# A hybrid decoder trunk on one core: input scaled chunk by chunk, time steps from the normalised input, the residual transposed in eight later jobs

## The chip, the cores and the metric

The kernel runs on one core of a Trainium2 chip. TensorE (PE) multiplies and transposes, VectorE (DVE), ScalarE (ACT) and GpSimd (POOL) work elementwise, and SyncE (SP) issues most of the DMA transfers; sixteen DMA engines carry them. The metric is the device time of one execution in microseconds.

## The reference

The trunk has two layers; only the first is touched. It adds 16 learned meta tokens in front of 1024 tokens (together 1040) of width 1024, normalises, and runs a state-space mixer:

```
h = jnp.concatenate([meta_tokens, x], axis=1)
u = h * rsqrt(mean(h * h) + 1e-6) * ssd_norm
z, xbc, dt_raw = jnp.split(u @ w_in, [2048, 2048 + 3072], axis=-1)
xbc = jax.nn.silu(_causal_dwconv(xbc, conv_w, conv_b))
xs, b_in, c_in = jnp.split(xbc, [2048, 2048 + 512], axis=-1)
dt = jax.nn.softplus(dt_raw + dt_bias)
a_cs = cumsum(dt * -exp(a_log))
y = ssd(xs, b_in, c_in, dt, a_cs)        # 32 heads in 4 groups, by chunks
h = h + gated_norm(y + xs * d_skip, z) @ w_out
```

A convolutional feed-forward block, a stick-breaking attention with one shared key and value, and a second feed-forward block follow, then a final normalisation that drops the meta tokens.

## The kernel before

Activations lie transposed: features on the 128 partitions (eight blocks, `KD`), tokens along the free axis. Tokens come in nine chunks `CH` of 116 (the last 112), and three token tiles `TT` of 348, 348 and 344, so one tile is three chunks. A product of fp32 operands is three float32r products of split operands (`mm3`, L193 high by high, L194 high weights by low input, L195 low weights by high input). `load_w` loads a 128x1024 block of weights on SyncE's queue (L174) into a buffer tagged `w32`, ScalarE rounds it to the high part `wh` (L180), GpSimd makes the low part `wl` in pieces (L98). All three tags rotate among three buffers.

`load_x` is the front. It starts the loads of the nine chunks, alternately on ScalarE's and SyncE's queue, and of the time-step weights, which GpSimd multiplies by the gain of the norm (L349). `stream(j)` handles the raw tile j: sums of squares (L364 on VectorE, L366 on ScalarE), raw transposes `xT` (L371) of three chunks for each feature block, copies of them into the residual `h` (L374, L376), a plain fp32 product `dtr` of time-step weights and raw residual (L377), and for the last tile the stores of eight residual blocks to HBM, `h_d` (L379). `token_rstd` makes the tile's factors 1/rms (L244 to L250). `scaled(j)` multiplies the chunks by the factors (L388), transposes them again (`xr`, L393) and splits them into the high and low parts `uh` (L303, ScalarE) and `ul` (L304, VectorE). `ORD` gives the program's order, tile by tile: `stream(j)`, then `scaled(j)`.

`dt_path` then finishes the time steps, multiplying the raw product by the factors at L460, and works out the decays. Its last step writes cumulated decays and their exponentials as rows to HBM, `acs_d` and `ea_d` (L499), from where each chunk of the state-space part loads them spread over partitions: `D` (L637, 116 partitions) and `E` (L643, 128 partitions).

`in_group(0)` projects the first group: six blocks of 128 columns (four of x, one of B, one of C), each for three token tiles, so 18 projections `pj` of 24 products, each followed by a convolution of four taps (L320 ScalarE, L323 VectorE) and a Silu (L512). `self.stream` walks through blocks and tiles and asks for a block's weights one block ahead. Up to here a list scheduler with a simulated timeline sets the order on each engine, from the program's dependences and tile pools; DMA issues stand on SyncE in the order it finds and one behind another, a waiting one in front of all later ones. From the next line on (`manual_schedule` in `mixer`) the order is written by hand. The first instructions of that part on TensorE are the transposes `cb` (L665) of chunk 0; they mark the end of the region that the change touches. The residual stored at the front is read again after the mixer.

Of the kernel before, what the change touches and what calls it, by code (L numbers as in the profile page):

```python
# [13 lines left out]
P = 128  # L14
# [54 lines left out]
LPOOL = ((2, 2), (2, 4), (2, 6), (2, 7))  # L69
ORD = ((0, 0), (1, 0), (0, 1), (1, 1), (0, 2), (1, 2))  # L70
XB, SQD = 9, (1, 4, 7)
# [29 lines left out]
class Trunk:  # L101
    def __init__(self, ctx, tc, a):
        self.tc, self.nc, self.a = tc, tc.nc, a
        nc = self.nc
        self.cp = ctx.enter_context(tc.tile_pool(name="cp", bufs=1))
        self.qp = ctx.enter_context(tc.tile_pool(name="qp", bufs=NQ))
        self.tmps = ctx.enter_context(tc.tile_pool(name="up", bufs=8))
        self.wp = ctx.enter_context(tc.tile_pool(name="wp", bufs=3))
        self.mp = ctx.enter_context(tc.tile_pool(name="mp", bufs=2, space=bass.MemoryType.PSUM))
        self.sp = ctx.enter_context(tc.tile_pool(name="sp", bufs=SMB, space=bass.MemoryType.PSUM))  # L110
        self.dp = ctx.enter_context(tc.tile_pool(name="dp", bufs=1, space=bass.MemoryType.DRAM))
        self.n = 0
        self.open = []
        self.consts()

# [55 lines left out]
    def load_w(self, src, n, gain=None, out=None):  # L171
# [7 lines left out]
        wh, wl = out or [self.wp.tile([P, 1024], F32R, tag=t, name=self.nm(t)) for t in ("wh", "wl")]  # L179
        nc.scalar.activation(wh[:, :n], w32[:, :n], AF.Copy)  # L180
        pieces(nc.gpsimd, wl[:, :n], w32[:, :n], wh[:, :n].bitcast(F32), ALU.subtract)
# [8 lines left out]
    def mm3(self, out, wh, wl, uh, ul, first, last, joins=False, tie=None):  # L190

        mm = self.nc.tensor.matmul
        self.behind(mm(out, wh, uh, start=first, stop=False, skip_group_check=joins), tie, "behind the sums of squares")  # L193
        mm(out, wh, ul, start=False, stop=False, skip_group_check=joins)  # L194
        mm(out, wl, uh, start=False, stop=last, skip_group_check=joins)  # L195

# [40 lines left out]
    def token_rstd(self, ss, m, k, eps=EPS, y=None, src=None):  # L237
# [3 lines left out]
        if y is None:  # L241
            y = self.small("ty")
            self.ln_exp()
        nc.vector.tensor_scalar(ss[:m, :k], (ss if src is None else src)[:m, :k], 1.0 / D, eps, op0=ALU.mult, op1=ALU.add)  # L244
        nc.scalar.activation(y[:m, :k], ss[:m, :k], AF.Ln)
        nc.scalar.activation(y[:m, :k], y[:m, :k], AF.Exp, scale=-0.5)
        nc.vector.tensor_tensor(b[:m, :k], y[:m, :k], y[:m, :k], op=ALU.mult)
# [47 lines left out]
    def parts(self, t, u, s0, n, g, eng=None):  # L295
# [6 lines left out]
        else:  # L302
            nc.scalar.activation(h, t, AF.Copy, scale=g)  # L303
            nc.vector.scalar_tensor_tensor(l, t, g, h.bitcast(F32), op0=ALU.mult, op1=ALU.subtract)  # L304

# [20 lines left out]

    def load_x(self, pool, mx):

# [3 lines left out]
        nc.vector.memset(ss, 1.0)  # L332
        wdt = self.wp.tile([P, 1024], F32, tag="w32", name="wdt")
        self.ln_exp()
        d = self.dp.tile([KD, P, L], F32, tag="h0_d", name="h0_d")
        r9 = mx.tile([P, 3, 3], F32, tag="r9", name="r9")
        dt = self.ex("dtr")
        xs = []
        for c, (t0, n) in enumerate(CH):
            xt = pool.tile([P, D], F32, tag="x", name=self.nm("x"), bufs=XB)  # L340
# [3 lines left out]
            else:  # L344
                self.by_rows(nc.sync if c % 2 else nc.scalar, xt[:n, :], a["x"][t0 - META : t0 - META + n, :], n)
            if c == 0:
                nc.sync.dma_start(wdt[:, : KD * H], a["w_dt"])
                v = wdt[:, : KD * H].rearrange("p (k h) -> p k h", k=KD)
                nc.gpsimd.tensor_tensor(v, v, self.par("ssd_norm", 0, KD).unsqueeze(2).to_broadcast([P, KD, H]), op=ALU.mult)  # L349
# [4 lines left out]
        hs = [self.Q("h") for _ in range(KD)]  # L354

        def stream(j):
            s0, nn = TT[j]
            x3 = xs[3 * j : 3 * j + 3]
            for i in range(3):
                c = 3 * j + i  # L360
                n = CH[c][1]
                t = self.wp.tile([P, D], F32, tag="wl", name=self.nm("junk"))
                if c in SQD:
                    nc.vector.scalar_tensor_tensor(t[:n, :], x3[i][:n, :], 1.0, x3[i][:n, :], op0=ALU.mult, op1=ALU.mult, accum_out=ss[:n, c : c + 1])  # L364
                else:
                    nc.scalar.activation(t[:n, :], x3[i][:n, :], AF.Square, accum_out=ss[:n, c : c + 1])  # L366
            for k in range(KD):
                ps = self.lg("xT")
                for i in range(3):
                    n = CH[3 * j + i][1]  # L370
                    nc.tensor.transpose(ps[:, i * CB : i * CB + n], x3[i][:n, k * P : k * P + P], self.ident[:n, :n])  # L371
                h = hs[k][:, s0 : s0 + nn]
                if k % 2:
                    nc.scalar.activation(h, ps[:, :nn], AF.Copy)  # L374
                else:
                    nc.vector.tensor_copy(h, ps[:, :nn])  # L376
# [3 lines left out]
            self.token_rstd(ss[:, 3 * j : 3 * j + 3], CB, 3, y=r9[:, :, j])  # L380

        def scaled(j):
            s0, nn = TT[j]
            x3 = xs[3 * j : 3 * j + 3]
            for i, t in enumerate(x3):
                n = CH[3 * j + i][1]
                r = r9[:n, i : i + 1, j]
                nc.vector.tensor_scalar(t[:n, :], t[:n, :], r, None, op0=ALU.mult)  # L388
            for k in range(KD):
                ps = self.sm("xr")  # L390
                for i in range(3):
                    n = CH[3 * j + i][1]
                    nc.tensor.transpose(ps[:, i * CB : i * CB + n], x3[i][:n, k * P : k * P + P], self.ident[:n, :n])  # L393
                self.parts(ps[:, :nn], u[k], s0, nn, self.par("ssd_norm", k))

        for step, j in ORD:
            (scaled if step else stream)(j)
        return d, u, dt, r9

# [33 lines left out]

    def dt_path(self, ps, r9, cp):

        nc, a = self.nc, self.a
        H, C = HEADS, 9 * HEADS
        heads = cp.tile([P, 2, H], F32, tag="heads", name="heads")
        nc.gpsimd.dma_start(heads.rearrange("p i h -> p (i h)"), a["heads"].to_broadcast([P, 2 * H]))
        aneg = heads[:, 1]  # L440
        self.tc.keep_in_program_order(nc.scalar.activation(aneg, aneg, AF.Exp))
        nc.vector.tensor_scalar(aneg, aneg, -1.0, None, op0=ALU.mult)

# [59 lines left out]
    def in_block(self, u, col, cv, out):  # L503
# [3 lines left out]
        def tile(w, j):  # L507
# [3 lines left out]
            self.conv(ps, t, n, 4, HALO, lambda i: self.par("ssd_conv_w", cv * 4 + i), self.par("ssd_conv_b", cv), self.settle)  # L511
            self.open.append(lambda: nc.scalar.activation(t, t, AF.Silu))  # L512

# [83 lines left out]
    def settle(self):  # L597

        todo, self.open = self.open, []
        for f in todo:  # L600
            f()

    def stream(self, blocks, w0=None):

# [10 lines left out]
        for n in range(3 * len(todo)):  # L615
            i, j = divmod(n, 3)
            if j == 0:
                if i + 1 < len(todo):
                    w.append(self.load_w(todo[i + 1][0], D))
                cur = w.pop(0)  # L620
            if n in calls:
                calls.pop(n)()
# [96 lines left out]
    def mixer(self, mx):  # L719


        with self.tc.tile_pool(name="start", bufs=3) as pool:
            hd, u, *dt = self.load_x(pool, mx)
            dt = self.dt_path(*dt, mx)
        with self.tc.tile_pool(name="ssd", bufs=3) as pool:
            yd, rows = [None] * 4, [[] for _ in range(4)]
            accs = [{} for _ in range(4)]
# [25 lines left out]
            with self.tc.manual_schedule(engines={E.PE, E.DVE, E.Activation, E.Pool}):  # L753
# [42 lines left out]
                for _ in work:  # L796
                    pass
        return hd, rows[3][:4], yd, list(zip(y0[1], y0[0]))

# [1031 lines left out]
```

## Time and profile before

| | us |
|---|---|
| median of 3 runs | 2890.64 |
| lowest and highest run | 2889.72, 2891.4 |
| the profiled execution | 2892.33 |
| its span | 2890.5 |

| instant in the profiled execution | us |
|---|---|
| first transpose of the input | 5.78 |
| first projection (L193) | 32.78 |
| transposes of the decay rows (L493) | 99.74 |
| first load of `D` issued | 103.59 |
| first transpose of the state-space part (L665) | 131.18 |

The profile is of one execution. A timeline row has the start, the length, the engine, line and operation, output and inputs, shapes and the number of instructions merged in the row, and in brackets the idle time of the engine before it and what ended it. A group row has the busy time and the mean ns of one instruction. SPq and ACTq rows are issues of DMA transfers; a row that merges several lasts from the first to the last.

### The profile page before, as it was taken

How to read it: one execution, taken by the hardware profiler on the slowest of the kernel's cores; microseconds unless marked ns; L12 is line 12 of the kernel's file. 1: busy time of each engine (PE TensorE's matmuls, PEld its weight loads, DVE VectorE, ACT ScalarE, POOL GpSimd, SP SyncE). 2: the span in 40 equal slices, each digit the busy share in tenths (PEclk: the TensorE clock that was granted, in tenths of full speed). 3: DMA queues.
4: the chain of work that ended last, by engine and by line, in shares of the span. 5: the costliest groups of instructions: out<-in, count | busy, mean ns of one | idle time of the engine just before them, and what ended most of it. 6: DMA issues, size and time to landing. Idle time of an engine off the chain costs nothing. (4 is left out here: it accounts for less than half of the span.)

```text
span 2890.5 us, 58592 instructions
## 1 busy us (share of the span) xinstructions
PE 2834.6 (98%) x21835; PEld 2701.9 (93%) x21835; DVE 2096.3 (73%) x4044; ACT 1628.0 (56%) x3392; POOL 1610.4 (56%) x2430
## 2 busy tenths in 40 slices
PE   7999999999999999999999999999999999999998
PEld 4999999999999999999999999999798999999888
DVE  5676666668387667666886888888749776767776
ACT  4455544544265656565335888888736565555433
POOL 2265555552429888858743222222363888885882
PEclk9999999999999999999999999999999999999999
DMA  5233333343213222244132222222332222225331
GB/s 168 75 107 95 117 94 117 114 156 135 81 60 97 81 81 76 81 161 164 52 114 78 57 68 66 62 63 54 134 117 74 81 76 79 81 81 183 110 102 66
DMA packets 128265, 278.70 MB, mean 96 GB/s; under 512 B 14787, under 2 KB 58828, under 8 KB 127980
## 3 DMA queue, kind: packets, MB, share of 16 engines
q1 hardware_dynamic: 122028, 261.70, 28.7%
q10 hardware_dynamic: 4112, 6.56, 0.7%
q0 software_dynamic: 1840, 6.70, 0.6%
q8 instruction: 172, 2.82, 0.4%
q14 instruction: 113, 0.93, 0.1%
HBM read 204.63 MB, written 55.36 MB: 90 GB/s over the span
## 5 line engine op out<-in xcount | busy, mean ns | idle before, releaser
L98 POOL TENSOR_TENSOR wl<-w,wh 128x256 fp32r<-128x256 f32 x768 | 682.0, 918 | 377.3 <-ACT wh L180 299.8
L193 PE MATMUL pj<-uh,wh 128*128 128x348 f32 (+2 forms) x1536 | 500.0, 326 | 2.7 <-DVE qs L1469 1.9
L194 PE MATMUL pj<-ul,wh 128*128 128x348 f32 (+2 forms) x1536 | 494.7, 322 | 0.0
L195 PE MATMUL pj<-uh,wl 128*128 128x348 f32 (+2 forms) x1536 | 491.5, 320 | 0.0
L193 PE MATMUL p<-bh,fh 128*128 128x262 f32 (+1 forms) x1408 | 400.4, 285 | 5.5 <-DVE p L1118 5.5
L195 PE MATMUL p<-bh,fl 128*128 128x262 f32 (+1 forms) x1408 | 400.1, 284 | 1.9 <-POOL fl L98 1.9
L194 PE MATMUL p<-bl,fh 128*128 128x262 f32 (+1 forms) x1408 | 398.7, 283 | 0.0
L98 POOL TENSOR_TENSOR fl<-x,fh 128x256 fp32r<-128x256 f32 x352 | 265.6, 786 | 191.9 <-ACT fh L1055 161.5
L193 PE MATMUL p<-bh,wh 128*128 128x262 f32 (+1 forms) x1040 | 295.7, 284 | 1.5 <-ACT ft L1115 1.5
L194 PE MATMUL p<-bl,wh 128*128 128x262 f32 (+1 forms) x1040 | 295.8, 284 | 1.2 <-DVE bl L979 1.2
L195 PE MATMUL p<-bh,wl 128*128 128x262 f32 (+1 forms) x1040 | 295.0, 284 | 0.0
L193 PEld LDWEIGHTS pj<-uh,wh 128*128 128x128 f32 x1536 | 288.3, 188 | 5.0 <-issue 1.9
L194 PEld LDWEIGHTS pj<-ul,wh 128*128 128x128 f32 x1536 | 288.9, 188 | 1.1
L195 PEld LDWEIGHTS pj<-uh,wl 128*128 128x128 f32 x1536 | 288.6, 188 | 0.6 <-issue 0.6
L323 DVE SCALAR_TENSOR_TENSOR c<-p,params,c 128x260 f32<-128x260 f32 (+1 forms) x528 | 248.5, 480 | 53.3 <-ACT c L320 46.7
L193 PEld LDWEIGHTS p<-bh,fh 128*128 128x128 f32 x1408 | 267.1, 190 | 6.3 <-DVE p L1118 5.9
L195 PEld LDWEIGHTS p<-bh,fl 128*128 128x128 f32 x1408 | 267.0, 190 | 2.8 <-POOL fl L98 2.5
L194 PEld LDWEIGHTS p<-bl,fh 128*128 128x128 f32 x1408 | 267.5, 190 | 0.1
L1115 ACT ACTIVATE ft<-p 128x262 f32<-128x262 f32 (+1 forms) x352 | 132.5, 382 | 175.0 <-DVE p L1118 111.2
L195 PE MATMUL acc<-gh,wl 128*128 128x260 f32 (+1 forms) x672 | 213.5, 320 | 2.8 <-POOL wl L98 2.6
L193 PE MATMUL acc<-gh,wh 128*128 128x260 f32 (+1 forms) x672 | 210.9, 320 | 3.1 <-DVE h L1279 3.1
L194 PE MATMUL acc<-gl,wh 128*128 128x260 f32 (+1 forms) x672 | 213.9, 319 | 0.0
(332 smaller groups left out, 7898.9 us busy)
## 6 DMA issues: line engine op xcount, KB each, us to landing
w<-in_w_up SPq DMA_DIRECT2D x88, 512.0 KB
w<-in_w_down SPq DMA_DIRECT2D x44, 512.0 KB
w<-in_w_in SPq DMA_DIRECT2D x40, 512.0 KB
E<-ea_d SPq DMA_DIRECT2D x32, 464.0 KB
D<-acs_d SPq DMA_DIRECT2D x32, 420.5 KB
g<-c SPq DMA_DIRECT2D x88, 130.0 KB
g<-c SPq DMA_DIRECT2D x88, 128.0 KB
b<-g SPq DMA_DIRECT2D x16, 520.0 KB
```

Of the source, the lines that this page charges most:

```text
L98: eng.tensor_tensor(out[:, c], x[:, c], y[:, c], op=op)
L193: self.behind(mm(out, wh, uh, start=first, stop=False, skip_group_check=joins), tie, "behind the sums of squares")
L194: mm(out, wh, ul, start=False, stop=False, skip_group_check=joins)
L195: mm(out, wl, uh, start=False, stop=last, skip_group_check=joins)
L323: ins = nc.vector.scalar_tensor_tensor(out, ps[:, o + i : o + i + n], wcol(i), out, op0=ALU.mult, op1=ALU.add)
L1115: nc.scalar.activation(s[:, :N], ps[:, :N], AF.Copy)
```

## The change

- The loads of the input stand on SyncE's queue but for chunks 0 and 2, which ScalarE issues. The first weight block is loaded between chunk 1 and the time-step weights.
- `tile(j)` takes the place of `stream` and `scaled`: the sums of squares of a chunk, factors of the first two chunks of a tile and then of the third, scaling chunk by chunk (the last chunk half on VectorE, half on ScalarE), transposes and parts. Squares of the next tile stand between the transposes of this one.
- Raw transposes, their copies into `h`, the plain product `dtr`, the gain on the time-step weights, the eight early stores and the multiplication by factors in `dt_path` go.
- The time steps come from the normalised parts by `mm3`, 24 triples of 96 columns with padded weights `wd`, in one bank.
- The meta tokens' columns of the residual are transposed at the start and stored.
- `residual(f)` makes the other 1024 columns of feature block f: it loads column block f of the input as 128x8x128 into a `w32` buffer, transposes eight times, copies the two banks back into the same buffer on ScalarE, and stores them to HBM. Eight such jobs are called, one after each of the projections 3, 5, ... 17 (counted from zero).
- The first three projections are interleaved with the tiles; some ties (`hold`, `copy_tie`, `silu_tie`, `last_mm`) only order instructions of one engine. The second block's weights are asked for one tile later.

```diff
-        for c, (t0, n) in enumerate(CH):
+        def load(c):
...
-                self.by_rows(nc.sync if c % 2 else nc.scalar, xt[:n, :], a["x"][t0 - META : t0 - META + n, :], n)
+                self.by_rows(nc.scalar if c == 2 else nc.sync, xt[:n, :], a["x"][t0 - META : t0 - META + n, :], n)
...
+        for c in range(3):
+            load(c)
+        w32 = self.wp.tile([P, 1024], F32, tag="w32", name="w32_0")
+        nc.sync.dma_start(w32, first)
...
+        nc.sync.dma_start(wdt, a["w_dt"])
+        for c in range(3, 9):
+            load(c)
...
+        def tile(j):
+            a, b, c = range(3 * j, 3 * j + 3)
+            if j == 0:
+                for x in (a, b, c):
+                    square(x, None)
+            factors(j, 0, 2)
+            scale(a, [(nc.vector, 0, D)])
+            factors(j, 2, 1)
+            scale(b, [(nc.scalar if j else nc.vector, 0, D)], None if j else self.first_factor)
+            if j == 0:
+                self.behind(nc.scalar.activation(w0[0], w32, AF.Copy), self.last_exp, "behind the factors")
+                pieces(nc.gpsimd, w0[1], w32, w0[0].bitcast(F32), ALU.subtract)
+            scale(c, [(nc.vector, 0, D // 2), (nc.scalar, D // 2, D)])
+            transposed(j, range(KD // 2))
...
+            transposed(j, range(KD // 2, KD))
...
-                nc.tensor.matmul(dt[j * H : j * H + H, :nn], wdt[:, k * H : k * H + H], h, start=k == 0, stop=k == KD - 1)
-                if j == 2:
-                    nc.sync.dma_start(d[k], hs[k][:, :L])
...
+                    self.mm3(dt[:G, :n], wd[0][:, w], wd[1][:, w], u[k][0][:, c], u[k][1][:, c], j == k == 0, j == 2 and k == KD - 1, tie=self.last_mm)
...
+    def residual(self, f):
+        nc = self.nc
+        t = self.wp.tile([P, 1024], F32, tag="w32", name=self.nm("xb"))
+        nc.sync.dma_start(t.rearrange("p (c q) -> p c q", q=P), self.a["x"][:, f * P : f * P + P].rearrange("(c p) q -> p c q", p=P))
+        banks = [self.sm("xT") for _ in range(2)]
+        for c in range(SEQ // P):
+            nc.tensor.transpose(banks[c // 4][:, c % 4 * P : c % 4 * P + P], t[:, c * P : c * P + P], self.ident)
+        for i, ps in enumerate(banks):
+            nc.scalar.activation(t[:, 512 * i : 512 * i + 512], ps, AF.Copy)
+        nc.sync.dma_start(self.h0_d[f, :, META:], t)
...
-        tt(v3, pv[R].rearrange("p (c h) -> p c h", h=H), r9[:CB].rearrange("p i j -> p (i j)").unsqueeze(2).to_broadcast([CB, 9, H]), op=ALU.mult)
-        tt(v3, v3, bias, op=ALU.add)
+        tt(v3, pv[R].rearrange("p (c h) -> p c h", h=H), bias, op=ALU.add)
...
-            for n, _ in enumerate(self.stream(into(0))):
+            blocks_left = iter(range(KD))
+            for n, _ in enumerate(group, 3):
+                if n % 2:
+                    for f in islice(blocks_left, 1):
+                        self.residual(f)
```

On SyncE, before, the loads of `D` and `E` and the weights behind the decay rows stand so (`w_176`, `w_196`, `w_223` are weights of later groups):

```order
L499 DMA acs_d<-rows_642 32x3x116 x3
L499 DMA ea_d<-ea_889 32x3x116 x3
L637 DMA D_1201<-acs_d 116x928
L637 DMA D_1299<-acs_d 116x928
L643 DMA E_1301<-ea_d 128x928
L174 DMA w_176_1384<-in_w_in 128x1024
L637 DMA D_1424<-acs_d 116x928
L643 DMA E_1426<-ea_d 128x928
L174 DMA w_196_1550<-in_w_in 128x1024
L174 DMA w_223_1770<-in_w_in 128x1024
```

In the changed kernel the same stretch of SyncE holds three residual loads (`xb_1098` to `xb_1258`, the sixth to the eighth), stores of residual blocks, and weights (`w_125` of the group's last block, `w_135` of the first block of the next group):

```order
L174 DMA w_125_1028<-in_w_in 128x1024
L707 DMA D_1276<-acs_d 116x928
L471 DMA h_d<-xb_938 128x1024
L707 DMA D_1374<-acs_d 116x928
L713 DMA E_1376<-ea_d 128x928
L707 DMA D_1499<-acs_d 116x928
L471 DMA h_d<-xb_1013 128x1024
L713 DMA E_1501<-ea_d 128x928
L465 DMA xb_1098<-in_x 128x8x128
L174 DMA w_135_1143<-in_w_in 128x1024
L465 DMA xb_1183<-in_x 128x8x128
L471 DMA h_d<-xb_1098 128x1024
```

The loads of the decay rows, which stood behind weights fetched earlier, now stand ahead of the sixth residual load and of the weights that the last projection before the state-space part uses.

On TensorE, before, the last projection ends and the state-space part begins:

```order
L193 MATMUL pj_1213<-uh_151,wh_1100 128x352
L194 MATMUL pj_1213<-ul_152,wh_1100 128x352
L195 MATMUL pj_1213<-uh_151,wl_1101 128x352
L665 MATMUL cb_1251<-ident,xbc_1007 116x128
L666 MATMUL cb_1251<-xbc_1107,xbc_1007 116x116
```

In the changed kernel the last projection (`pj_1288`) begins behind the transposes of the sixth residual load and holds those of the seventh:

```order
L195 MATMUL pj_1228<-uh_153,wl_1031 128x348
L468 MATMUL xT_1100<-ident,xb_1098 128x128 x4
L468 MATMUL xT_1101<-ident,xb_1098 128x128 x4
L193 MATMUL pj_1288<-uh_139,wh_1145 128x352
L194 MATMUL pj_1288<-ul_140,wh_1145 128x352
L468 MATMUL xT_1185<-ident,xb_1183 128x128 x4
L195 MATMUL pj_1288<-uh_139,wl_1146 128x352
```

and it ends with those of the eighth, in front of the first transpose of the state-space part:

```order
L194 MATMUL pj_1288<-ul_154,wh_1145 128x352
L195 MATMUL pj_1288<-uh_153,wl_1146 128x352
L468 MATMUL xT_1260<-ident,xb_1258 128x128 x4
L468 MATMUL xT_1261<-ident,xb_1258 128x128 x4
L735 MATMUL cb_1326<-ident,xbc_1037 116x128
```

Three of the eight residual jobs have thus moved in among the last rows ahead of the state-space part.

More of the change, by code (lines that the diff above doesn't have):

```diff
@@ L179, in load_w @@
         wh, wl = out or [self.wp.tile([P, 1024], F32R, tag=t, name=self.nm(t)) for t in ("wh", "wl")]
-        nc.scalar.activation(wh[:, :n], w32[:, :n], AF.Copy)
+        self.behind(nc.scalar.activation(wh[:, :n], w32[:, :n], AF.Copy), self.copy_tie, "behind the tiles in front")
         pieces(nc.gpsimd, wl[:, :n], w32[:, :n], wh[:, :n].bitcast(F32), ALU.subtract)
@@ L194, in mm3 @@
         mm(out, wh, ul, start=False, stop=False, skip_group_check=joins)
-        mm(out, wl, uh, start=False, stop=last, skip_group_check=joins)
+        self.last_mm = mm(out, wl, uh, start=False, stop=last, skip_group_check=joins)
     def split(self, t, s, eng=None, tiles=TT):
@@ L382, in scaled @@
[L382 to L394, printed above, removed]
@@ L396, in load_x, with square @@
-        for step, j in ORD:
-            (scaled if step else stream)(j)
-        return d, u, dt, r9
+        G = 3 * H
+        wd = [self.Q("wd", F32R) for _ in range(2)]
+        for t in wd:
+            nc.gpsimd.memset(t.bitcast(F32), 0.0)
+        taps = [t[:, 2 * H : 2 * H + KD * G].rearrange("p (k h) -> p k h", h=G)[:, :, :H] for t in wd]
+        made = {}
+        def square(c, tie):
+            n = CH[c][1]
+            t = self.wp.tile([P, D], F32, tag="wl", name=self.nm("junk"))
+            x, acc = xs[c][:n, :], ss[:n, c : c + 1]
+            if c in SQD:
+                ins = nc.vector.scalar_tensor_tensor(t[:n, :], x, 1.0, x, op0=ALU.mult, op1=ALU.mult, accum_out=acc)
+            else:
+                ins = nc.scalar.activation(t[:n, :], x, AF.Square, accum_out=acc)
+            self.behind(ins, tie, "behind the tile in front")
@@ new lines, in load_x, with factors, scale @@
+        heads = mx.tile([P, 2, H], F32, tag="heads", name="heads")
+        nc.gpsimd.dma_start(heads.rearrange("p i h -> p (i h)"), a["heads"].to_broadcast([P, 2 * H]))
+        def factors(j, i, n):
+            self.token_rstd(ss[:, 3 * j + i : 3 * j + i + n], CB, n, y=r9[:, i : i + n, j])
+        def scale(c, parts, tie=None):
+            n = CH[c][1]
+            r = r9[:n, c % 3 : c % 3 + 1, c // 3]
+            for eng, c0, c1 in parts:
+                x = xs[c][:n, c0:c1]
+                if eng is nc.vector:
+                    self.behind(eng.tensor_scalar(x, x, r, None, op0=ALU.mult), tie, "behind the last factors' sums")
+                else:
+                    eng.activation(x, x, AF.Copy, scale=r)
@@ new lines, in transposed @@
+        def transposed(j, ks):
+            s0, nn = TT[j]
+            for k in ks:
+                ps = self.sm("xr")
+                for i, x in enumerate(xs[3 * j : 3 * j + 3]):
+                    n = CH[3 * j + i][1]
+                    t = nc.tensor.transpose(ps[:, i * CB : i * CB + n], x[:n, k * P : k * P + P], self.ident[:n, :n])
+                    if j:
+                        self.behind(t, self.last_mm, "behind the products in front")
+                made[j, k] = self.parts(ps[:, :nn], u[k], s0, nn, self.par("ssd_norm", k))
@@ new lines, in load_x, with steps @@
+        pm = self.lg("mT")
+        for k in range(KD):
+            nc.tensor.transpose(pm[:, k * META : k * META + META], xs[0][:META, k * P : k * P + P], self.ident[:META, :META])
+        mt = self.tmp("mT")[:, : KD * META]
+        nc.scalar.activation(mt, pm[:, : KD * META], AF.Copy)
+        nc.sync.dma_start(self.h0_d[:, :, :META].rearrange("k p c -> p k c"), mt.rearrange("p (k c) -> p k c", c=META))
+        dt = self.lg("dtr")
+        def steps():
+            tile(0)
+            w = wdt.rearrange("p (k h) -> p k h", h=H)
+            self.behind(nc.scalar.activation(taps[0], w, AF.Copy), made[0, 0][0], "behind the first tile")
+            nc.gpsimd.tensor_tensor(taps[1], w, taps[0].bitcast(F32), op=ALU.subtract)
+            self.behind(nc.scalar.activation(heads[:, 1], heads[:, 1], AF.Exp), made[0, KD - 1][0], "behind the first tile")
+            nc.vector.tensor_scalar(heads[:, 1], heads[:, 1], -1.0, None, op0=ALU.mult)
+            self.hold = True
+            yield
+            for j in range(3):
+                s0, n = TT[j]
+                c = slice(HALO + s0, HALO + s0 + n)
+                for k in range(KD):
+                    w = slice(2 * H + G * k - H * j, 2 * H + G * k - H * j + G)
+                    self.mm3(dt[:G, :n], wd[0][:, w], wd[1][:, w], u[k][0][:, c], u[k][1][:, c], j == k == 0, j == 2 and k == KD - 1, tie=self.last_mm)
+                if j < 2:
+                    tile(j + 1)
+                    self.copy_tie = made[1, 3 + 4 * j][0]
+                else:
+                    self.hold = None
+                self.silu_tie = self.last_exp
+                yield
@@ L722, in mixer @@
         with self.tc.tile_pool(name="start", bufs=3) as pool:
-            hd, u, *dt = self.load_x(pool, mx)
-            dt = self.dt_path(*dt, mx)
+            u, dt, heads, w0, front = self.load_x(pool, mx, self.a["w_in"][DI // P])
+            dt = self.dt_path(dt, heads, mx)
+            next(front)
+            rows = [[] for _ in range(4)]
+            group = self.stream(self.in_group(u, 0, rows[0]), w0, True)
+            for _ in range(3):
+                next(group)
+                next(front)
+            next(dt)
         with self.tc.tile_pool(name="ssd", bufs=3) as pool:
-            yd, rows = [None] * 4, [[] for _ in range(4)]
+            yd = [None] * 4
             accs = [{} for _ in range(4)]
```

69 lines of the change are left out of this document (25 added, 44 removed).

## The prediction

> **What bounds the kernel now.** I read the page's first part, then the busy time by stretches of the start, then TensorE's timeline there, SyncE's issues and the DMA share.
>
> ```profile
> PE 2834.6 (98%) x21835; PEld 2701.9 (93%) x21835; DVE 2096.3 (73%) x4044; ACT 1628.0 (56%) x3392; POOL 1610.4 (56%) x2430
> 5.78:32.78 27.00, 17.74 (x66) 7.24 (x66) 13.81 (x30) 12.53 (x28) 7.48 (x9) 1.00 0.72 196
> 32.78:60.00 27.22, 27.15 (x160) 17.93 (x159) 17.13 (x32) 12.96 (x24) 2.80 (x4) 1.00 0.50 197
> 60.00:131.18 71.18, 70.04 (x438) 67.80 (x437) 40.24 (x78) 35.69 (x60) 14.53 (x21) 1.00 0.28 80
> ```
>
> TensorE is busy 98% of the span. Each stretch shows its length, then PE, PEld, DVE, ACT and POOL busy, the granted clock, the DMA share and GB/s. TensorE lacks 9.3 us of the first 27.0; from the first projection (32.78) to the first transpose of the state-space part (131.18, "the marker") it is full. The change ends before or at the marker, and what follows has the same work in both, so I forecast the marker and carry its shift to the end.
>
> ```profile
> 19.24 0.84 PE L371 MATMUL xT<-ident,x 116*128 116x116 f32 x3
> 21.31 0.84 PE L371 MATMUL xT<-ident,x 116*128 116x116 f32 x3
> 26.06 0.52 PE L371 MATMUL xT<-ident,x 116*128 116x116 f32 x3
> 27.21 0.52 PE L371 MATMUL xT<-ident,x 116*128 116x116 f32 x3
> 32.78 0.40 PE L193 MATMUL pj<-uh,wh 128*128 128x352 f32 x1
> 130.85 0.32 PE L194 MATMUL pj<-ul,wh 128*128 128x352 f32 x1
> 131.01 0.33 PE L195 MATMUL pj<-uh,wl 128*128 128x352 f32 x1
> 131.18 0.27 PE L665 MATMUL cb<-ident,xbc 128*116 128x128 f32 x1
> 131.49 0.60 PE L669 MATMUL px<-ident,xbc 128*116 128x128 f32 x4
> 131.84 0.41 PE L193 MATMUL pj<-uh,wh 128*128 128x352 f32 x1
> 65.80 0.46 PE L393 MATMUL xr<-ident,x 116*128 116x116 f32 x3
> 66.60 0.46 PE L393 MATMUL xr<-ident,x 116*128 116x116 f32 x3
> ```
>
> Starts of neighbours give prices. A float32r product takes 0.16 (130.85 to 131.01), so a projection of one block and token tile (24 products) 3.84. Four 128x128 transposes take 0.35 (131.49 to 131.84), 0.0875 each. Three transposes of the scaled input with three products between them take 0.80, so 0.32 without. Three raw transposes and their plain time-step product take 1.15 (26.06 to 27.21), but 2.07 while TensorE still waits often (19.24 to 21.31).
>
> **What goes.** 24 groups of raw transposes and time-step products at 1.15 = 27.6 us of TensorE, and eight stores of the residual at the start. **What comes on TensorE.** 72 products for the time steps at 0.16 = 11.5 and 64 residual transposes at 0.0875 = 5.6. The marker still has 19 projections ahead of it (18 of the group, one of the next), 73.0; 24 transposed triples, 7.7; and about 2.0 of time-step path. So 110.3 becomes 99.8, 10.5 less.
>
> **When the projections start.**
>
> ```profile
> 11.35 1.01 PE L371 MATMUL xT<-ident,x 116*128 116x116 f32 x4 [4.95 <-DMA x<-in_x]
> 12.64 1.22 DVE L364 SCALAR_TENSOR_TENSOR junk<-x 116x1024 f32<-116x1024 f32 x1
> 15.36 1.06 ACT L366 ACTIVATE junk<-x 116x1024 f32<-116x1024 f32 x1 [13.27 <-DMA x<-in_x]
> 17.58 0.17 DVE L244 TENSOR_SCALAR ss<-ss 116x3 f32<-116x3 f32 x1 [0.41 <-ACT junk L366]
> 19.88 0.16 DVE L250 TENSOR_TENSOR r<-r,tb 116x3 f32<-116x3 f32 x1
> 40.77 1.41 DVE L388 TENSOR_SCALAR x<-x,r 116x1024 f32<-116x1024 f32 x2 [0.57 <-PE xT L371]
> L303 ACT ACTIVATE uh<-xr,params 128x348 fp32r<-128x348 f32 (+1 forms) x24 | 12.5, 549 | 9.4 <-PE xr L393 9.3
> ```
>
> Chunk 1 lands by 11.35, or about 10.4 without the time-step weights ahead of it. Its square takes 1.3, factors about 1.45 (17.58 to 20.04 is 2.46, with one ACT square of 1.04 between), one scale 0.70, the second factors and half scale about 2.0, transposes 0.4, the first high part 0.55: from 10.4 that is 16.8, so the first projection starts near 17.5, 15.3 us earlier. Work to the marker was 110.3, of which 98.4 lay after 32.78; now nearly all 99.8 lies after 17.5. Early products are at the slow pitch: of some 6 us, 6 x (1 - 1.15/2.07) = 2.7 is lost. Waits of the second and third tile on ACT and DVE I put at 3 (bounds 0, and 7 from the 9.3 missing before). With no wait for a DMA the marker falls at 17.5 + 99.8 - 0.5 + 2.7 + 3 = 122.5, 8.7 earlier. That is the promise.
>
> **What the moved transfers do.** All now share SyncE's queue: eight residual loads (1024 pieces of 512 B each), eight stores, and weights. The load buffers rotate among three, shared with the weights.
>
> ```profile
> 103.59 0.70 SPq L637 DMA_DIRECT2D D<-acs_d  x2
> 104.78 0.40 SPq L174 DMA_DIRECT2D w<-in_w_in  x1
> 105.22 0.53 SPq L637 DMA_DIRECT2D D<-acs_d  x1
> 141.70 0.27 SPq L637 DMA_DIRECT2D D<-acs_d  x1
> DMA  0000022222222222222222222222222220000000
> q1 hardware_dynamic: 120, 0.43, 17.3%
> q1 hardware_dynamic: 145, 0.52, 25.6%
> 61.23 0.33 SPq L174 DMA_DIRECT2D w<-in_w_in  x1
> q1 hardware_dynamic: 144, 0.52, 40.7%
> q1 hardware_dynamic: 376, 1.43, 88.9%
> q1 hardware_dynamic: 448, 0.18, 40.2%
> q1 hardware_dynamic: 576, 0.53, 25.8%
> ```
>
> The DMA row is 142 to 148 us, in slices of 0.15, where one load of D (decay rows spread to 116 partitions) is alone. It runs 28 slices = 4.2 us at a quarter share: four of sixteen engines carry it. The queue rows (packets, MB, share) are of 142 to 148, 118 to 123, 61 to 65, 45 to 49, 102.5 to 104.5 and 911 to 917. In 118 to 123 the share is again a quarter, 15 us after the loads of D were issued. Counting from 105, three D at 4.2, two E at 1.6 x 464/512 = 1.45 and two weight loads at 1.6 (40.7% of 4 us, 26 engine-us over 16) are 18.7 us, to 123.7: so four engines serve the ring in order and carry a backlog, while twelve are empty. Before, nobody needs what stands behind it; the weights are fetched far ahead.
>
> In the new order the residual's sixth load stands behind all three D, and TensorE's transposes of it stand, in order, in front of the last projection. Block 5's weights (1.6), three D (12.6), two E (2.9) and two residual stores (1.3 each: 88.9% of 4 us over 1.43 MB, by 0.52) are 19.7. The group starts 3.7 earlier than before (the products and transposes ahead of it end near 96 instead of 99.74), 101.3; I take 102, since block 5's weights first wait for a residual store. So the four engines are free at 121.7.
>
> A residual load on one engine is 64 pieces. The nearest row is 464-byte packets: 40.2% of 2 us x 16 / 448 = 28.7 ns, by 512/464 = 31.7, so T = 2.0. Bounds: 64 x 28.7 = 1.8; 64 x 48 (25.8% of 6 x 16 / 576, packets of 1040 B) = 3.1 as the upper row. The Trainium skill ("DMA: Bandwidth & Descriptors", Specifications) has full rate from 512 B on; by it T would be the weight load's 1.6 and the marker 0.8 earlier.
>
> The sixth load lands at L = 121.7 + 2.0 + 0.4 = 124.1. TensorE wants it at 122.5 less one projection (3.84) and 24 transposes (2.1): 116.5, so it stands some 7.5 us. The chain does not end there:
>
> ```profile
> L180 ACT ACTIVATE wh<-w 128x1024 fp32r<-128x1024 f32 x8 | 8.4, 1056 | 7.2 <-PE pj L195 4.7 <-PE pj L194 2.6
> L98 POOL TENSOR_TENSOR wl<-w,wh 128x256 fp32r<-128x256 f32 x32 | 24.0, 783 | 90.1 <-ACT wh L180 90.1
> ```
>
> Block 6's weights land at L + 1.6; high part 1.06, at L + 2.7; low part 4 x 0.783, L + 5.8. The seventh load lands at L + 3.6. The eighth needs the buffer that the weights leave, is issued at L + 5.9 behind a store, and lands after 3.4 (3.0 from issue to landing of the load at 61.23, by T in place of 1.6) and about 0.5 of that store: L + 9.8. Eight transposes and the wait's end make L + 10.9: marker at 135.0, 3.8 later than before. T enters twice: 134.6 to 137.2.
>
> Behind the marker the next weights come late too, about 1.0 more, as they wait for a residual store. After such idle stretches TensorE's first products ran at the slow pitch; 0 (no idle long enough) to 2.7 (6 us of it), I take 1.3. The sum is +3.8 + 1.0 + 1.3 = +6.1. The Trainium skill ("TensorE: Matmul & The Clock Gate", Part 1) has half clock after some 3.4 us without work and about as long to recover; by it the waits of 7.5 and of 5 would each cost up to 1.7, 3.4 in place of 1.3. The pair 2.07 against 1.15 agrees in kind.
>
> The profiled execution's own span is 2890.5 and its time 2892.33, 1.8 around it; the median of the runs is 2890.64, 1.7 lower. Span 2890.5 + 6.1 = 2896.6, and by the median 2890.64 + 6.1 = **2896.7**. With bounds (T 1.8 to 3.1, slow pitch 0 to 2.7, tile waits hidden under the stall, group start 101.3 to 104): 2892 to 2902.
>
> **Rivals.** A, the backlog does not bind: residual loads pass the D loads, or D lands before the sixth load is wanted. Then the marker is at 122.5, and 2890.64 - 8.7 = 2882. For it: the 10.5 less work is sure, and twelve engines are empty. Against it: the quarter share at 118 to 123. The Trainium skill (the same page on DMA, "Queues, rings and completion order") has descriptors of one engine and queue start in their order; by it A needs the backlog to be smaller. Chance 0.17.
>
> B, the 512-byte pieces are dear: a strided read costs about 100 ns (twice the upper row), T = 6.4. Each of eight loads then takes that long on all engines, L moves by 4.4 and the eighth load by as much: near 2905. It decides from about 70 ns. For it: no row of before reads such pieces. Against it: 1040-byte packets at 48. Chance 0.13.
>
> C, the front comes later than worked out: the first weights are split behind squares on ACT, the second block's load comes a tile late, the tiles wait 4 us more than my 3, and these delays push the rows of D, and all behind them, by about 4: 2901. Against it: the first 27 us have 14 us free on ACT and 13 on DVE. Chance 0.10.
>
> The forecast has 0.60. What this kernel's measurement can tell from no change is 0.2%, 5.8 us. Of the forecast's 0.60, 0.27 lies below 2896.4 and 0.33 above; A gives 0.13 faster and 0.04 same; B and C are 0.22 slower and 0.01 same. Faster 0.13, same 0.32, slower 0.55. The range leaves out half of A's lower side and B's upper: 2883 to 2907.
>
> **What would show it.** First projection near 17.5. Loads of D from about 102 at a quarter share to about 122. TensorE idle before the residual transposes, released by a DMA of the residual's load, 7 us at the sixth and about 5 at the eighth, with the high part of block 6's weights waiting for their load; marker near 135. Wrong: no idle there and the marker at 122 to 124 (A); residual loads at over 70 ns a piece (B); the first projection after 21 (C); or a shift at the marker that later waits take back or double.

## The result and the profile after

| | us |
|---|---|
| changed kernel, median of 5 runs (lowest to highest) | 2902.61 (2897.04 to 2907.14) |
| kernel before, median of 5 runs | 2889.93 (2886.82 to 2891.4) |
| ratio, 95% interval | 1.0042 (1.0028 to 1.0057) |
| span of the profiled execution, before and after | 2890.5, 2900.7 |

The change makes the kernel 0.42% slower, 12.7 us by the medians, 10.2 us by the two spans. The first view of the changed kernel is the busy time by stretches: length, then PE, PEld, DVE, ACT and POOL busy, granted clock, DMA share, GB/s.

```profile
16.80:32.00 15.20, 14.45 (x77) 13.12 (x77) 10.59 (x28) 10.21 (x23) 2.21 (x4) 1.00 0.72 199
32.00:100.00 68.00, 67.81 (x447) 66.36 (x445) 38.50 (x82) 42.80 (x75) 11.80 (x17) 1.00 0.23 72
100.00:113.00 13.00, 10.04 (x50) 9.44 (x50) 3.85 (x7) 5.08 (x8) 2.81 (x4) 0.87 0.71 230
113.00:139.20 26.20, 16.57 (x98) 15.53 (x97) 5.21 (x9) 6.44 (x12) 2.82 (x4) 0.87 0.57 175
```

To 100 us the new front keeps TensorE nearly full. Then come 39 us in which it lacks 12.6 us, and in which the granted clock is 0.87 on average: what is left runs slower too. TensorE's timeline (start, length, operation, idle time before and what ended it) shows where:

```profile
16.82 0.66 PE L193 MATMUL pj<-uh,wh 128*128 128x352 f32 x1 [0.25 <-ACT uh L303]
94.63 0.46 PE L561 MATMUL rows<-ident,cols 116*96 116x116 f32 x3
106.76 0.43 PE L193 MATMUL pj<-uh,wh 128*128 128x352 f32 x1 [2.06 <-ACT wh L180]
108.94 0.49 PE L193 MATMUL pj<-uh,wh 128*128 128x352 f32 x1
109.23 0.49 PE L194 MATMUL pj<-ul,wh 128*128 128x352 f32 x1
128.06 1.97 PE L468 MATMUL xT<-ident,xb 128*128 128x128 f32 x8 [7.35 <-DMA xb<-in_x]
130.47 0.66 PE L193 MATMUL pj<-uh,wh 128*128 128x352 f32 x1 [0.45 <-ACT wh L180]
138.19 1.07 PE L468 MATMUL xT<-ident,xb 128*128 128x128 f32 x8 [1.84 <-DMA xb<-in_x]
139.10 0.27 PE L735 MATMUL cb<-ident,xbc 128*116 128x128 f32 x1
150.22 1.12 PE L765 MATMUL S<-xde,bk 116*128 116x512 f32 x2 [2.51 <-DVE xbc L323]
152.22 0.32 PE L735 MATMUL cb<-ident,xbc 128*116 128x128 f32 x1
```

The first projection starts at 16.82 instead of 32.78, the decay rows are transposed at 94.63 instead of 99.74. The gain is there, 5.1 us by then with part of the residual's transposes already done. It goes in four waits and in products at a slower pitch behind them: 2.06 for the weights of the group's last block, 7.35 for the sixth residual load, 0.45 for the high part of block 6's weights (blocks counted from zero, so the first block of the next group), 1.84 for the eighth residual load. The rows at 108.94 and 109.23 are 0.29 apart where neighbours were 0.16: the slow pitch. The marker comes at 139.10 instead of 131.18, 7.9 later. The second `cb` comes at 152.22, where the kernel before has it at:

```profile
141.59 0.32 PE L665 MATMUL cb<-ident,xbc 128*116 128x128 f32 x1
```

That is 10.6 later, and 10.2 of it are left at the end, by the two spans. SyncE's issues in the changed kernel show what stood in the queue, and two rows of the DMA queue how long it moved: 118 to 122 us, then 66 to 71 us, where one residual load is alone (packets, MB, share).

```profile
100.97 0.36 SPq L174 DMA_DIRECT2D w<-in_w_in  x1
101.38 0.33 SPq L707 DMA_DIRECT2D D<-acs_d  x1
102.13 0.33 SPq L707 DMA_DIRECT2D D<-acs_d  x1
102.93 0.40 SPq L707 DMA_DIRECT2D D<-acs_d  x1
111.98 0.38 SPq L465 DMA_DIRECT2D xb<-in_x  x1
112.47 9.77 SPq L174 DMA_DIRECT2D w<-in_w_in  x1
125.20 0.38 SPq L465 DMA_DIRECT2D xb<-in_x  x1
133.40 0.38 SPq L465 DMA_DIRECT2D xb<-in_x  x1
...
q1 hardware_dynamic: 110, 0.40, 25.9%
q1 hardware_dynamic: 998, 0.50, 34.1%
```

The sixth residual load is issued at 111.98 and lands 16 us later; between 118 and 122 only a quarter of the engine time is used, by 110 packets, nearly all as large as a row of D or E (3712 bytes). One residual load alone costs 34.1% of 5 us x 16 = 27.3 engine-us for 998 packets, 27 ns each, so it isn't slow by itself.

### The profile page after: what moved, and what is told of

It is laid out like the page before. It is cut to its first block, busy times and chain, and to the rows that moved or that the text cites. A ratio compares the mean times of both kernels' runs of the same rounds, so it can differ in the third digit from the quotient of the medians.

```text
span 2900.7 us, 58687 instructions
## 1 busy us (share of the span) xinstructions
PE 2832.8 (98%) x21859; PEld 2716.9 (94%) x21859; DVE 2087.1 (72%) x4044; ACT 1639.0 (57%) x3411; POOL 1622.8 (56%) x2432
## 3 DMA queue, kind: packets, MB, share of 16 engines
q10 hardware_dynamic: 3712, 5.15, 0.5%
## 4 chain that ended last, share of the span: by engine, by line
PE 44%; DVE 2%; ACT 2%; POOL 1%; issue 1%; DMA 0%; ACTq 0%; DVEq 0%; SPq 0%; POOLq 0%
PE p L195 5%; PE p L193 5%; PE p L194 5%; PE acc L193 4%; PE acc L195 4%; PE acc L194 4%; PE pj L193 3%; PE pj L194 3%; PE pj L195 3%; PE po L1640 3%; PE lg L1599 3%; PE wT L1626 3%; POOL wl L97 1%; ACT kp L1602 0%; DVE h L1053 0%
## 5 line engine op out<-in xcount | busy, mean ns | idle before, releaser
L323 DVE SCALAR_TENSOR_TENSOR xbc<-pj,params,xbc 128x348 f32<-128x348 f32 (+1 forms) x216 | 124.4, 577 | 128.2 <-ACT xbc L320 123.4
```

What stands on the lines that cost most here:

```text
L323: ins = nc.vector.scalar_tensor_tensor(out, ps[:, o + i : o + i + n], wcol(i), out, op0=ALU.mult, op1=ALU.add)
```

## The experiments

Each was timed with the kernel before on the same chip. The median of before was 2892.07 for the first four, 2892.43 for the next four, 2890.36 for the last.

| kernel | median us | ratio to before, 95% interval | marker us |
|---|---|---|---|
| changed, first three D split | 2890.89 | 0.9998 (0.9989 to 1.0006) | 130.46 |
| before, first three D split | 2891.34 | 0.9996 (0.9987 to 1.0004) | 130.44 |
| changed, residual loads of whole rows | 2901.96 | 1.0037 (1.0025 to 1.0049) | 136.43 |
| the new front alone | 2876.13 | 0.9950 (0.9938 to 0.9962) | 115.56 |
| own buffers | 2895.02 | 1.0013 (1.0004 to 1.0022) | 132.44 |
| own buffers, D split | 2886.32 | 0.9976 (0.9967 to 0.9985) | 122.91 |
| own buffers, early jobs | 2883.96 | 0.9974 (0.9964 to 0.9984) | 121.03 |
| own buffers, early jobs, D split | 2885.09 | 0.9975 (0.9966 to 0.9984) | 121.43 |
| early jobs, shared buffers | 2902.97 | 1.0041 (1.0027 to 1.0055) | 143.73 |

**The changed kernel with the first three D loads split.**

```diff
-        nc.sync.dma_start(dk, self.acs_d[c, h0 : h0 + GH].unsqueeze(0).to_broadcast([n, GH, CB]))
+        src = self.acs_d[c, h0 : h0 + GH].unsqueeze(0)
+        if g == 0 and c < 3:
+            for r0, r1 in ((0, 112), (112, n)):
+                nc.sync.dma_start(dk[r0:r1], src.to_broadcast([r1 - r0, GH, CB]))
```

> The changed kernel, but the first three loads of the decay rows D are each issued as 112 rows and 4 rows. Theory (D runs on four engines, and the sixth residual load queues behind it in the ring): 112 rows spread over all sixteen engines, so a D load takes 7 packets an engine at 138 ns plus a short tail, some 1.1 us instead of 4.2; the ring is 9 us shorter, the sixth residual load lands near 116 instead of 128.1, TensorE does not wait for it or for the eighth, the first transpose of the state-space part comes near 126 instead of 139.1, and the whole falls by 12 to 15 us to 2888 to 2891. Rival (the 512-byte pieces of the residual loads are dear): the wait at the sixth load shrinks by no more than 4 us, to 2898 or more. Rival (the load buffers shared with the weights set the chain): the sixth load is issued and lands late all the same, 2900 or more.

The time is as the theory had it, some 12 us less (2890.89 against 2902.61, ratios 0.9998 and 1.0042), by an edit that moves the same bytes on more engines. TensorE no longer waits for the sixth load; for the eighth it still does, which the theory had not, and the marker comes at 130.46 instead of the expected 126. That the time is in the range all the same is in part luck: some 3 us more come back behind the marker (8.6 at the marker, 11.5 by the spans). TensorE's timeline, then three of SyncE's issues, then the low part of block 6's weights on GpSimd:

```profile
120.32 1.04 PE L468 MATMUL xT<-ident,xb 128*128 128x128 f32 x8
128.73 1.94 PE L468 MATMUL xT<-ident,xb 128*128 128x128 f32 x8 [2.64 <-DMA xb<-in_x]
130.46 0.42 PE L740 MATMUL cb<-ident,xbc 128*116 128x128 f32 x1
...
109.81 1.63 SPq L174 DMA_DIRECT2D w<-in_w_in  x1
122.59 0.33 SPq L471 DMA_DIRECT2D h_d<-xb  x1
123.65 0.38 SPq L465 DMA_DIRECT2D xb<-in_x  x1
...
120.81 2.81 POOL L97 TENSOR_TENSOR wl<-w,wh 128x256 fp32r<-128x256 f32 x4 [11.02 <-ACT wh L180]
```

The eighth load stands behind the store of the sixth job (122.59), which waits for that job's transposes at 120.32 and its copies, and it needs the buffer that block 6's weights leave: their low part ends at 123.62, and the load is issued at 123.65. So with shared buffers it comes late even when the engines are free.

**The kernel before with the same split.**

> The kernel before, with the same split of the first three D loads. Theory: before, nothing that stands behind these loads in the ring is wanted soon, so the time stays at 2890 within 3 us, although the engines are free some 9 us earlier. If the quarter-share loads cost the kernel before something too, it is over 3 us faster.

No change of time. The DMA share in 112 to 120 us (slices of 0.2, tenths), of the split kernel and then of the kernel before, shows that the split did free the engines:

```profile
DMA  9989999999999710000000000003000000000000
...
DMA  9799999957799997992222213232222721232232
```

The ring is empty near 115 instead of running on at a quarter, and nobody was waiting for it. The slow loads of D were there before; the change put work that is wanted behind them.

**Residual loads of whole rows.**

```diff
-        nc.sync.dma_start(t.rearrange("p (c q) -> p c q", q=P), self.a["x"][:, f * P : f * P + P].rearrange("(c p) q -> p c q", p=P))
+        nc.sync.dma_start(t, self.a["x"][f * P : f * P + P, :])
```

> The changed kernel, but each residual load reads 128 whole rows of the input (4 KB pieces, same bytes, same place in every queue) instead of a column block in 512-byte pieces; the residual then holds other numbers, so this kernel computes another result. Theory (pieces of 512 B cost 2.0 us a load on one engine against 1.6): the sixth load lands 0.5 earlier, the time falls by 1 us, to 2901 to 2902. Rival (512-byte pieces are dear, 100 ns each): each load is 5 us shorter on every engine, the time falls by 9 us or more, to 2893 or less.

TensorE's wait at the sixth load is 7.70 instead of 7.35, and ends 1.4 earlier:

```profile
126.69 1.97 PE L468 MATMUL xT<-ident,xb 128*128 128x128 f32 x8 [7.70 <-DMA xb<-in_x]
136.43 0.27 PE L735 MATMUL cb<-ident,xbc 128*116 128x128 f32 x1
```

The first load of D is issued 1.4 earlier too:

```profile
100.01 0.33 SPq L707 DMA_DIRECT2D D<-acs_d  x1
...
q1 hardware_dynamic: 144, 0.52, 35.5%
```

From that issue to the end of the wait it takes 26.68 us (100.01 to 126.69), and in the changed kernel 26.68 as well (101.38 to 128.06). The queue row is of one load of whole rows alone, in 66 to 71 us: 35.5% where the load in pieces had 34.1%. Dear pieces are out. The marker is 2.7 earlier than in the changed kernel, but the time is the same within the scatter (ratios 1.0037 and 1.0042); 1.5 of the 2.7 are gone by the second `cb` (151.05 against 152.22), as the wait in front of the state's product is 3.41 instead of 2.51.

**The new front alone.** Each residual job is cut to one store of something that is there already.

```diff
-        t = self.wp.tile([P, 1024], F32, tag="w32", name=self.nm("xb"))
...
-        nc.sync.dma_start(self.h0_d[f, :, META:], t)
+        nc.sync.dma_start(self.h0_d[f, :, META:], self.uh[f][:, HALO + META : HALO + L].bitcast(F32))
```

> The changed kernel without the residual's loads, transposes and copies: each job only stores a block of the normalised input's high part in the residual's place, so the result is another one. It is the new front alone. By the changed kernel's own trace, 139.1 less 15 us of waits and slow pitch behind them, less 64 transposes at 0.0875 = 5.6, is 118.5 for the first transpose of the state-space part, 12.7 earlier than before; theory: the whole gain arrives, 2877 plus or minus 3. Rival (the gain of the front is given back later in the kernel): over 2884.

The marker comes 2.9 earlier than worked out, and the time is as expected, 0.50% below before: the gain of 15.6 us at the marker, without the residual's work, reaches the end of the kernel.

```profile
115.56 0.27 PE L729 MATMUL cb<-ident,xbc 128*116 128x128 f32 x1
```

**Own buffers for the residual.**

```diff
-        t = self.wp.tile([P, 1024], F32, tag="w32", name=self.nm("xb"))
+        t = self.Q("xb")[:, :1024]
```

> The changed kernel, but a residual job loads into a spare row buffer of its own pool instead of a buffer that the weights use. The weights then stand far ahead in SyncE's queue, and the sixth residual load stands ahead of the decay loads D; the seventh and eighth stand behind them, since they need a buffer back. Theory: no wait for weights any more and none at the sixth load; the seventh and eighth land when the four engines are through with D, near 125, and TensorE, which wants them near 119, waits 5 to 7 us once; time 2886 to 2892.

This missed, by 3 us above the upper end. The mechanism is the expected one: the only long wait is now at the seventh load, which lands at 125.63, as expected, but TensorE wants it at 117, not 119, and behind the wait the granted clock is 0.75 in 120 to 140.

```profile
125.63 1.97 PE L468 MATMUL xT<-ident,xb 128*128 128x128 f32 x8 [8.66 <-DMA xb<-in_x]
120.00:140.00 20.00, 14.37 (x84) 14.30 (x85) 5.74 (x16) 8.03 (x12) 1.56 (x2) 0.75 0.37 128
```

**Own buffers and the split.** Both edits.

> The same with the first three loads of D split into 112 and 4 rows. Theory: the seventh and eighth loads land near 115 to 117, before TensorE wants them; no wait left, time that of the front alone (2876.1) plus 64 transposes at 0.0875 (5.6), 2882 plus or minus 3. Rival (the residual jobs cost through something else than these waits, their copies on ScalarE or the stores): 2886 or more.

8.7 us less than with own buffers alone. The seventh load lands when it is wanted, with 0.23 of wait in the first row here, and the eighth with 0.51; the time is 1.3 above the expected range, and just at the rival's bound. The next two kernels differ from it in the place of the jobs and are 1.2 and 2.4 us faster, with scatters of 8 us and ratios (0.9974 to 0.9976) that are the same within their intervals; what is left of the rival wasn't followed.

```profile
117.48 1.09 PE L468 MATMUL xT<-ident,xb 128*128 128x128 f32 x8 [0.23 <-DMA xb<-in_x]
122.91 0.27 PE L740 MATMUL cb<-ident,xbc 128*116 128x128 f32 x1
```

**Own buffers and early jobs.** All loads then stand ahead of D, which is not split.

```diff
-                if n % 2:
+                if n >= 3:
```

> Own buffers, D not split, and a residual job after each projection from the fourth on instead of after every second: all eight loads stand ahead of D in the queue. Theory: D still takes its four engines until past 120, but nothing that TensorE wants stands behind it: 2882 plus or minus 3, like the kernel with the split. Rival (D's long loads slow TensorE's data in another way): 3 us or more above the kernel with own buffers and split.

The time is in the expected range, and its rival falls. With the kernels above and below it, the same within their intervals, this is the fastest version with the whole computation, 0.26% below before. From 100 us to its marker TensorE has no gap, at full clock; the third row, the DMA share in 116 to 122 us in slices of 0.15, shows that D still runs at a quarter there:

```profile
100.00:121.03 21.03, 21.03 (x139) 20.95 (x138) 9.36 (x17) 11.43 (x19) 4.51 (x7) 1.00 0.72 213
121.03 0.27 PE L735 MATMUL cb<-ident,xbc 128*116 128x128 f32 x1
...
DMA  9999999985444333322313212333222322222222
```

The marker is that of the front alone plus the 64 transposes (115.56 + 5.6 = 121.2), so ahead of it the residual's copies and stores cost nothing more.

**The same with the split.**

> Own buffers, early jobs and D split. Theory: with nothing wanted behind D, the split is worth nothing, within 3 us of the kernel with own buffers and early jobs; 2882 plus or minus 3.

Within 1.2 us of the kernel without it, and 0.1 above the expected range: where nothing is wanted behind D, the split is worth nothing.

**Early jobs, buffers still shared.**

> The changed kernel with a residual job after each projection from the fourth on, but with the load buffers still shared with the weights. All eight residual loads then stand ahead of D, and instead the group's last weights (and those of the next group) stand behind the first two loads of D. Theory (whatever TensorE wants behind D in the ring waits, whether residual or weights): TensorE, through with the fifth block near 108, waits for the last block's weights until they have landed behind two D, near 113 to 116, plus 1.1 for their high part; 8 to 10 us are lost in all, 2892 to 2902. Rival (it is the place of the residual loads that costs): no wait near the end, 2882 plus or minus 3, like the kernel with own buffers and early jobs.

It is as slow as the changed kernel, 1 us above the expected range, and not a single residual transpose waits for a load near the end. TensorE waits for weights in their stead:

```profile
81.35 0.43 PE L193 MATMUL pj<-uh,wh 128*128 128x352 f32 x1 [3.49 <-ACT wh L180]
104.18 0.66 PE L193 MATMUL pj<-uh,wh 128*128 128x352 f32 x1 [5.36 <-ACT wh L180]
125.92 0.66 PE L193 MATMUL pj<-uh,wh 128*128 128x352 f32 x1 [5.40 <-ACT wh L180]
...
109.19 0.38 SPq L174 DMA_DIRECT2D w<-in_w_in  x1
...
124.81 1.06 ACT L180 ACTIVATE wh<-w 128x1024 fp32r<-128x1024 f32 x1 [7.73 <-DMA w<-in_w_in]
```

The last wait is the one of the theory: weights issued at 109.19 behind two loads of D are there at 124.8, 9 to 12 us later than the 113 to 116 that I had worked out. The other two, 8.85 us together, were not foreseen: the residual loads take the three shared buffers, and the weights are loaded late (those for the wait at 104.18 are issued only at 98.18, behind the stores of two residual blocks). So the time is near the range partly for another reason than the theory's, and that it equals the changed kernel's is chance; the last wait alone bears the theory out. Neither early jobs alone nor own buffers alone bring the kernel below the one before: with the first the weights stand behind D, with the second the seventh load.

## Why the prediction was right, and where it was off

The sign, the place and the mechanism were right, and the time lay in the range of 2883 to 2907, 6 us above the forecast of 2896.7. The size was not: 12.7 us instead of 6.1, and 0.6 above the bounds of 2892 to 2902 that the forecast's own terms gave. The wider range was made for the rivals, which all fell.

- **The front.** First projection forecast near 17.5, measured 16.82. The marker without any wait, forecast at 122.5, is 121.03 in the kernel with own buffers and early jobs. The kernel with the front alone shows that this gain isn't lost later. Rival C falls.
- **The backlog.** Loads of D at a quarter share from about 102: measured between 118 and 122 (25.9%), issued from 101.38. Splitting them takes the wait of 7.35 away. Rival A falls.
- **The pieces.** Forecast 31.7 ns, measured 27 where a load was alone, so T is 64 x 27 = 1.7 instead of 2.0, and whole rows save nothing from the issue of D to the sixth load. Rival B falls. The upper row was also misread: 25.8% of 6 x 16 over 576 packets is 43 ns, and 48 only over the 512 of them that are not tiny; that moves a bound, not the forecast. The Trainium skill ("DMA: Bandwidth & Descriptors", Specifications) has full rate from 512 B on. By it a load would take the 1.6 of a weight load, and the trace's 1.7 agrees: here the page was the better guide.
- **The sixth load.** This is the term that was mis-sized: L was forecast at 124.1 and is 128.06. The sum took packets of D, E and weights as fast beside others as alone. The trace shows that D's are slower. In 113 to 117 the first 768 of the sixth load's 1024 pieces move on the engines that are free, and beside them, in 114 to 116, come 30 large packets, 15 a us, where 118 to 122 has 106, 26.5 a us:

```profile
DMA packets 554, 0.38 MB, mean 188 GB/s; under 512 B 7, under 2 KB 524, under 8 KB 554
q1 hardware_dynamic: 554, 0.38, 108.8%
DMA packets 73, 0.19 MB, mean 377 GB/s; under 512 B 2, under 2 KB 30, under 8 KB 73
```

The first two rows are of 114 to 116. From 117 to 124 none of the pieces moves; the last row is of 124 to 124.5, where the last quarter begins, 28 pieces in that half microsecond. In the trace's packet records the last row of D or E starts at 125.64. By then only the four engines still have such rows. So the first of the four was free for the sixth load 2.3 us later than the forecast 121.7, and the last one 4.1 later; from there to L it took 2.3, against 2.4 in the sum (2.0 + 0.4). The backlog is the term that was too small, by 4 us, and other pieces of the load moved beside the very transfers that its last quarter waited for. Why D's packets are slower beside others wasn't tried. The same misjudgment shows in the last experiment, by some 9 us.

- **From L to the marker.** Forecast L + 10.9; 128.06 + 10.9 = 139.0, measured 139.10. That it fits to 0.1 is the sum of small errors: the high part of block 6's weights starts at 129.4 and the eighth load is issued at 133.40, L + 5.3 against L + 5.9, but it is 4.8 until TensorE has it, against 3.9.
- **TensorE's own need.** It was forecast to stand from 116.5 and stood from 120.7, for 7.35 instead of 7.5. The 2.06 wait for the weights of the group's last block and the slow pitch behind it weren't in the sum. That the wait has the forecast length is luck, two errors of 4 us that cancel; the marker hangs on L alone, so they cost nothing.
- **Behind the marker.** Forecast 1.0 for late weights and 1.3 for slow pitch, 2.3 in all; the spans show 10.2 - 7.9 = 2.3. The sum is hit, its parts are not: nearly all is one wait of 2.51 in front of the state's product in chunk 0, while the slow pitch lies ahead of the marker. The wait goes back to ScalarE, which starts the next convolution (L320) 2.4 us after the marker (141.55) instead of 0.2 (131.38 before): the copies of the eighth job and the next weights' high part come first, with only 0.50 of waiting for the weights' load. Nor can one profiled execution carry a tenth here: in the kernel with own buffers, early jobs and the split the shift is -9.75 at the marker and -5.2 at the end.
- **The median** moved by 12.7 and not by 10.2. The profiled execution of before took 2892.33, 2.4 above the median of its runs beside the changed kernel, and that is the difference.

## What to carry to other kernels

When an edit moves a load to another place in a queue, look at what stands ahead of it there and on how many engines that runs: a transfer on four of sixteen engines makes all that follows it in the ring wait for its length, whether it was cheap before or not. A kernel may carry such a transfer unpunished for as long as all later loads are fetched far ahead; buffers shared between the new loads and the weights take this lead away. And the slow transfer can get slower still beside others: here D's packets came at little more than half their rate while pieces of the sixth load moved on the other engines. The split of the slow loads alone took the loss against the kernel before away; to be faster than before took buffers of their own as well, and with these either the split or early loads were enough.

## What the runs showed of the hardware

- A wait of only 2.06 us on TensorE (104.70 to 106.76), with one of 0.33 behind it, was followed, 1.9 us after it ended, by products 0.29 apart instead of 0.16. The granted clock was half for 3.4 us there, and for 6.8 us around the end of the wait of 7.35:

```profile
108.50:111.90 3.40, 3.40 (x14) 3.40 (x13) 0.91 (x2) 0.49 (x1) 1.51 (x3) 0.50 0.84 307
125.56:132.39 6.83, 3.89 (x16) 3.42 (x17) 0.99 (x2) 2.97 (x6) 1.84 (x3) 0.50 0.34 104
```

The kernel with the split shows the first of these behind a wait of 1.83. A slow stretch thus doesn't need the several idle microseconds that the prediction had in mind. The Trainium skill ("TensorE: Matmul & The Clock Gate", Part 1: The HAM clock gate) asks for an idle window of about 3.4 us. Here a shorter wait was enough; the length of the first slow stretch agrees with the page.

- The issue of block 6's weights occupied SyncE's queue for 9.77 us in the changed kernel, from 112.47 until the quarter-share stretch ended. It took 1.63 us with D split, and 1.49 with D whole but residual loads of whole rows. So neither the backlog on four engines alone nor the 512-byte pieces alone made it last that long; what exactly stops the queue was not tried.
